# Moving a sample's recurrent-state update from ScalarE and VectorE to GpSimd

## The chip, the core and the metric

The kernel runs on one core of one Trainium2 chip. The number that counts is the device time of one launch in microseconds (us). Engines are named as the profile names them: PE is TensorE (PEld its weight loads), DVE is VectorE, ACT is ScalarE, POOL is GpSimd, SP is SyncE. Each engine runs its instructions in the order in which they stand in its queue; an instruction that waits for a semaphore holds back everything behind it on its engine.

## The reference, cut to what matters

One layer of a decoder step: 256 prompt tokens and 8 sample tokens share all weights. The mixer half has three branches; two of them (HGRN2 with 8 heads of 128x128, GLA with 4 heads of 128x256) are gated linear recurrences. For the samples there is one new token, so the recurrence is a single step from a given state:

```
S_t = diag(f_t) S_{t-1} + k_t v_t^T       # per sample and head; S is dk x dv
o_t = S_t^T q_t
```

Both the new state S_t (an output, for every sample and head) and o_t are wanted. The rest (norms, projections, an MLP, the prompt's recurrence in chunks) is matrix work over the 264 tokens.

## The kernel before, in words

**Main stream.** All projections are computed as weight-stationary matmuls in an fp32 scheme of three products (lines 602, 603, 604): each weight block `raw` is loaded by SP, rounded to `whi` by ACT (line 109) and its remainder `wlo` made by DVE (line 106, `wlo = raw - whi`, two SBUF inputs), then PE runs three 128x264 matmuls for each 128x128 block. The unit of the stream is the *granule*: 8 weight blocks of 128x128, so 24 matmuls on PE. `now` counts granules while the program is written out; the whole program has 578. Splits run two granules ahead, loads five.

**Side work.** Everything else in the mixer half is written between granules by generators that hand over after each piece: `mixer_r(G)` (queue `bg`) for the prompt's recurrence of a group G, and `samples_r(G)` (queue `bs`) for the samples of the same group. There are three groups, in this order: two HGRN halves (four heads each, dv = 128) and GLA (dv = 256). Small matmuls of the side work are gathered into *slots* between two granules: line 633 (prompt levels), line 640 (samples), line 342 (the modulation's weights).

**The samples' step.** `samples_r` goes through `steps`: 8 steps in an HGRN group (one per sample), 16 in GLA (two per sample). The tile of a step is 128x512 (`st`, the state; `vbc`, the value row, spread over all partitions from DRAM scratch `vs_d`). In each step:
- POOL issues the load of the state two steps ahead (line 1029, `fetch`; 4 buffers) and of the value row one step ahead (line 1035, `values`; 2 buffers);
- ACT scales the state by the decay `fs`, one instruction per head (line 1055);
- DVE adds the outer product, `st = v * k + st`, one instruction per head (line 1057), where the per-partition scalar is a column of `k` (`G.k`, a [128, 4, 264] tile);
- POOL issues the store of the state (line 1058);
- after a sample's last step, `samples.append((now[0], ...))`; `slot` takes it `AGE` = 2 granules later and writes its products `S_t^T q` (line 640) to PE.

With 4 state buffers, the load of step n+2 goes into the buffer of step n-2, so it waits until the product of that step has been read by PE.

**What reads k and who gets its buffer.** `k` is also read by the prompt's side, last in `mul(kd, kd, k[:, :, 0:NP])` (line 1170). Tiles `b` come from a pool of 28 buffers, and a buffer is given to a new tile when the last reader of the old one is done. In the built program of both kernels the tile `qd` of the first group (written by ACT's exponential at line 1163, multiplied by q on DVE in a `mul`, which the profile shows at its helper's line 100, and read by PE in the products at line 1176) lies at the same address as that group's `k`. Line 1176 stands on PE at granule 127 in both kernels.

**What sets the order.** PE, SP and POOL keep the order in which the program is written. For DVE and ACT a scheduler chooses it when the kernel is built, so a change of their work moves their other instructions as well.

Of the kernel before, what the change touches and what calls it, by code (L numbers as in the profile page):

```python
# [10 lines left out]
AF = mybir.ActivationFunctionType  # L11
ALU = mybir.AluOpType
# [3 lines left out]
P = 128  # L16
D = 2048
KT = D // P
NP = 256
# [32 lines left out]
FETCHED = 3  # L52
AGE = 2
ADA_LAND = 4


@with_exitstack
def hybrid_step_kernel(
# [8 lines left out]
    nc = tc.nc  # L67
    V, S, T = nc.vector, nc.scalar, nc.tensor
# [17 lines left out]
    def blk(shape=None, dt=F32):  # L86
        shape = shape or [P, 4, NT]
        return blkp.tile(shape, dt, tag="b", name=nm("b"))
# [4 lines left out]
    def tmp(shape, tag, bufs=2):  # L93
        return tp.tile(shape, F32, tag=tag, name=nm(tag), bufs=bufs)
# [4 lines left out]
    def mul(o, a, b):  # L99
        V.tensor_tensor(o, a, b, op=ALU.mult)  # L100
# [72 lines left out]
    def rstd_small(ms, scale, out):  # L173

        n, w = out.shape
        xx, aa = tmp([P, 16], "sx")[0:n, 0:w], tmp([P, 16], "sa")[0:n, 0:w]
        c = 0
        for m in ms if isinstance(ms, list) else [ms]:
            V.tensor_scalar(xx[:, c:c + m.shape[1]], m, scale, EPS, ALU.mult, ALU.add)
            c += m.shape[1]  # L180
        V.tensor_scalar(out.bitcast(I32), xx.bitcast(I32), -0.5, 1597463007.0, ALU.mult, ALU.add)
        for _ in range(3):
            mul(aa, out, out)
            V.scalar_tensor_tensor(aa, aa, -0.5, xx, ALU.mult, ALU.mult)
            V.scalar_tensor_tensor(out, aa, 1.5, out, ALU.add, ALU.mult)
# [102 lines left out]
    class Rounds:  # L288
# [27 lines left out]
        def due(self):  # L316
            if self.ws:
                return self.full() and now[0] >= self.at + ADA_LAND
            return self.done is not None and not self.todo and now[0] >= self.at + 2 * ADA_LAND

# [35 lines left out]
    now = [0]  # L356
# [250 lines left out]
    levels, samples = [], []  # L607
# [406 lines left out]
    def samples_r(G):  # L1014

        dv = G.dv
        nj, nh = dv // P, 512 // dv
        q, k, g = G.q, G.k, G.g
        fs = tmp([P, 4, NS], "fs")
        S.activation(fs, g[:, :, NP:NT], AF.Exp)  # L1020
        qm = blk([P, 4, NS, 32])
        mul(qm, q[:, :, NP:NT].unsqueeze(3).to_broadcast([P, 4, NS, 32]),
            delta.rearrange("p (b c) -> p b c", b=NS).unsqueeze(1).to_broadcast([P, 4, NS, 32]))
        steps = [(b, h) for b in range(NS) for h in range(0, 4, nh)]
        ahead, vals = [], []

        def fetch(b, h):
            st = tmp([P, nh, dv], "st", ST_BUFS)
            nc.gpsimd.dma_start(st, G.s_in(b, h, nh))
            ahead.append((st, now[0]))  # L1030

        def values(b, h):
            v = tmp([P, 4, P], "vbc", VB_BUFS)
            r0 = 4 * nj * b + h * nj
            nc.gpsimd.dma_start(v, vs_d[G.i, r0:r0 + 4, :].partition_broadcast(P))
            vals.append((v.rearrange("p (h j) v -> p h (j v)", h=nh), now[0]))

        for s in steps[0:2]:
            fetch(*s)
            yield  # L1040
        values(*steps[0])
        yield
        os_ = tmp([P, dv], f"os{G.i}", 1)
        sts = []
        for n, (b, h0) in enumerate(steps):
            if n + 2 < len(steps):

                yield lambda: len(sts) + sum(len(x[3]) for x in samples) <= ST_BUFS - 3
                fetch(*steps[n + 2])
            if n + 1 < len(steps):  # L1050
                values(*steps[n + 1])
            yield lambda: now[0] >= max(ahead[0][1] + FETCHED, vals[0][1] + FETCHED - 1)
            st, v = ahead.pop(0)[0], vals.pop(0)[0]
            for i in range(nh):
                S.activation(st[:, i, :], st[:, i, :], AF.Copy, scale=fs[:, h0 + i, b:b + 1])  # L1055
            for i in range(nh):
                V.scalar_tensor_tensor(st[:, i, :], v[:, i, :], k[:, h0 + i, NP + b:NP + b + 1], st[:, i, :], ALU.mult, ALU.add)  # L1057
            nc.gpsimd.dma_start(G.s_out(b, h0, nh), st)  # L1058
            sts.append(st)
            if h0 + nh == 4:  # L1060
                samples.append((now[0], (G, qm, os_), b, sts))
                sts = []
            yield
        yield lambda: not samples
        yield READY
        ss, rr = tmp([P, 1], "sss", 1), tmp([P, 1], "srr", 1)
        S.activation(tmp([P, dv], "vt"), os_, AF.Square, accum_out=ss)
        rstd_small(ss, 1.0 / dv, rr)
        S.activation(os_, os_, AF.Copy, scale=rr)
        G.os = os_  # L1070
        yield

    def mixer_r(G):
# [18 lines left out]
        q, k, g = G.q, G.k, G.g  # L1092

        bs.g.append(samples_r(G))


# [625 lines left out]
```

## Time and profile before

| | |
|---|---|
| time, median of 3 runs | 1942.22 us (1941.23 to 1944.57) |
| span of the profiled execution | 1942.9 us; no other time of that execution is given |
| PE busy | 1903.4 us (98%) |
| DVE busy | 1186.1 us (61%) |
| ACT busy | 1006.5 us (52%) |
| POOL busy | 83.9 us (4%), 142 instructions, most of them DMA issues |
| the samples' work, lines 1029 to 1058 and 640 | from 377 to 850 us of the span |

How to read it: "busy" is the union of the instructions of an engine. A wait is put down to the instruction that waits and to the last thing that it waited for. The chain of work that ended last is followed back from the last instruction; idle time of an engine that is not on it costs nothing. A clock of 1.00 is the full TensorE clock.

### The profile page before, as it was taken

Reading aid. Unit: us, or ns where it says so; the run is one execution under the profiler, and the core shown is the slowest. Engines: PE = TensorE matmul, PEld = TensorE weight load, DVE = VectorE, ACT = ScalarE, POOL = GpSimd, SP = SyncE. Lnnn points to the kernel's source line nnn. Section 1 sums busy time; section 2 is a strip of 40 time slices with the busy share of each in tenths; the row PEclk is TensorE's granted clock in tenths of the full one; section 3 lists DMA queues with packets and bytes.
Section 4 is the critical chain, followed back from the end, with each engine's and each line's share of the span. In section 5 each row is a group of like instructions: output and inputs, shape, how many; then the busy total and the mean of one; then the engine's idle time right before and its main releaser. Section 6 shows DMA issues by size and latency. Waiting matters only on the chain.

```text
span 1942.9 us, 42324 instructions
## 1 busy us (share of the span) xinstructions
PE 1903.4 (98%) x17080; PEld 1812.1 (93%) x17080; DVE 1186.1 (61%) x2103; ACT 1006.5 (52%) x1825; POOL 83.9 (4%) x142
## 2 busy tenths in 40 slices
PE   6999999998999999999999999999999999999998
PEld 5989999988999998999999988999999999999997
DVE  4566667686578695565555666545556555555665
ACT  5444454665666765544444556444444545454444
POOL 1000000001001112200000010000000000000000
PEclk9999999999999999999999999999999999999999
DMA  9897786688588688987777846776566555555552
GB/s 317 299 337 247 249 287 213 214 250 276 175 262 290 214 258 283 306 266 249 253 256 233 300 129 195 229 226 199 178 182 184 179 180 184 177 183 182 179 183 99
DMA packets 339380, 442.06 MB, mean 228 GB/s; under 512 B 14930, under 2 KB 281024, under 8 KB 339184
## 3 DMA queue, kind: packets, MB, share of 16 engines
q1 hardware_dynamic: 329120, 409.62, 65.5%
q0 software_dynamic: 8992, 28.48, 4.6%
q8 instruction: 134, 2.20, 0.5%
q10 hardware_dynamic: 1072, 1.25, 0.2%
q14 instruction: 62, 0.51, 0.1%
HBM read 427.60 MB, written 11.70 MB: 226 GB/s over the span
## 4 chain that ended last, share of the span: by engine, by line
PE 95%; DMA 2%; issue 1%; ACT 1%; DVE 1%; POOL 0%; SPq 0%; ACTq 0%; DVEq 0%; POOLq 0%
PE mm L602 29%; PE mm L603 29%; PE mm L604 28%; PE ada L342 3%; PE ada L274 1%; PE sm L633 1%; PE sm L780 1%; DMA raw<-in_w_in_dram 1%; PE sm L640 0%; DMA b<-in_x_prompt_dram 0%; DMA vbc<-vs_d 0%; DVE wlo L106 0%; DMA b<-in_w_ada_dram 0%; ACT gt L1515 0%; PE sm L1176 0%
## 5 line engine op out<-in xcount | busy, mean ns | idle before, releaser
L602 PE MATMUL mm<-b,whi 128*128 128x264 f32 x4624 | 1326.6, 287 | 7.5 <-ACT b L109 3.5
L603 PE MATMUL mm<-b,whi 128*128 128x264 f32 x4624 | 1317.8, 285 | 0.8 <-DVE b L106 0.8
L604 PE MATMUL mm<-b,wlo 128*128 128x264 f32 x4624 | 1314.5, 284 | 1.4 <-issue 0.7
L106 DVE TENSOR_TENSOR wlo<-raw,whi 128x512 fp32r<-128x512 f32 x1136 | 775.5, 689 | 572.0 <-ACT whi L109 570.0
L109 ACT CAST whi<-raw 128x512 fp32r<-128x512 f32 x1136 | 695.4, 618 | 730.6 <-PE mm L603 654.5
L602 PEld LDWEIGHTS mm<-b,whi 128*128 128x128 f32 x4624 | 872.3, 189 | 49.1 <-issue 26.2
L604 PEld LDWEIGHTS mm<-b,wlo 128*128 128x128 f32 x4624 | 872.5, 189 | 2.2 <-DVE wlo L106 1.1
L603 PEld LDWEIGHTS mm<-b,whi 128*128 128x128 f32 x4624 | 872.2, 189 | 1.4 <-DVE b L106 1.3
L103 DVE TENSOR_TENSOR b<-b,mm 128x528 f32<-128x528 f32 (+1 forms) x137 | 95.7, 700 | 42.7 <-PE mm L604 42.7
L1057 DVE SCALAR_TENSOR_TENSOR st<-vbc,b,st 128x128 f32<-128x128 f32 (+1 forms) x96 | 34.1, 389 | 51.1 <-DMA vbc<-vs_d 44.2
L1055 ACT ACTIVATE st<-st,fs 128x128 f32<-128x128 f32 (+1 forms) x96 | 37.0, 430 | 53.0 <-DMA st<-in_state_hgrn_dram 27.0
L274 PE MATMUL ada<-b,cT 128*32 128x256 f32 (+1 forms) x640 | 35.7, 361 | 7.2 <-DMA b<-in_w_ada_dram 7.0
L342 PE MATMUL ada<-araw,cT 128*32 128x512 f32 x296 | 39.9, 601 | 0.0
L274 PEld LDWEIGHTS ada<-b,cT 128*32 128x32 f32 x640 | 18.2, 115 | 19.7 <-issue 6.4
L100 DVE TENSOR_TENSOR b<-b,b 128x512 f32<-128x512 f32 (+1 forms) x47 | 34.1, 740 | 1.4 <-ACT b L1165 0.9
L1058 POOL DMA_DIRECT2D out_dram<-st x32 | 23.5, 735 | 156.6 <-DVE st L1057 150.8
L342 PE MATMUL ada<-b,cT 128*32 128x512 f32 x216 | 26.2, 593 | 0.0
L106 DVE TENSOR_TENSOR b<-gt,b 128x528 fp32r<-128x528 f32 x32 | 22.7, 708 | 3.9 <-ACT whi L109 0.9
L106 DVE TENSOR_TENSOR b<-b 128x1024 f32<-128x1024 f32 (+1 forms) x24 | 24.3, 1016 | 0.0
L109 ACT CAST whi<-araw 128x512 fp32r<-128x512 f32 x20 | 12.4, 621 | 20.7 <-PE mm L603 19.0
L100 DVE TENSOR_TENSOR gt<-vt 128x528 f32<-128x528 f32 x32 | 22.4, 701 | 0.9 <-ACT vt L1581 0.9
L1587 ACT ACTIVATE b<-vt 128x528 fp32r<-128x528 f32 x32 | 20.7, 647 | 1.0
(339 smaller groups left out, 825.2 us busy)
## 6 DMA issues: line engine op xcount, KB each, us to landing
raw<-in_w_in_dram SPq DMA_DIRECT2D x232, 512.0 KB, 4.7
raw<-in_w_mlp_up_dram SPq DMA_DIRECT2D x128, 512.0 KB, 3.7
raw<-in_w_mlp_down_dram SPq DMA_DIRECT2D x128, 512.0 KB, 3.6
b<-in_w_ada_dram SPq DMA_DIRECT2D x102, 512.0 KB, 6.4
araw<-in_w_ada_dram SPq DMA_DIRECT2D x74, 512.0 KB, 6.0
raw<-in_w_branch_dram SPq DMA_DIRECT2D x48, 512.0 KB, 4.5
raw<-in_w_out_dram SPq DMA_DIRECT2D x32, 512.0 KB, 3.9
b<-in_w_ada_dram SPq DMA_DIRECT2D x32, 256.0 KB, 5.7
```

What stands on the lines that cost most here:

```text
L100: V.tensor_tensor(o, a, b, op=ALU.mult)
L103: V.tensor_tensor(o, a, b, op=ALU.add)
L106: V.tensor_tensor(o, a, b, op=ALU.subtract)
L109: S.copy(hi, src)
L274: T.matmul(acc[32 * j:32 * j + 32, 0:n], cT[:, k, :], w[:, n * j:n * j + n], start=k == 0, stop=k == KT - 1)
L342: T.matmul(self.acc[32 * j:32 * j + 32, :], cT[:, k, :], ws[j // 2][:, j % 2 * 512:j % 2 * 512 + 512], start=k == 0, stop=k == KT - 1)
L602: T.matmul(o, a, xh(k + j), start=first and j == 0, stop=False)
L603: T.matmul(o, a, xl(k + j), start=False, stop=False)
L604: T.matmul(o, b, xh(k + j), start=False, stop=last and j == n - 1)
L1055: S.activation(st[:, i, :], st[:, i, :], AF.Copy, scale=fs[:, h0 + i, b:b + 1])
L1057: V.scalar_tensor_tensor(st[:, i, :], v[:, i, :], k[:, h0 + i, NP + b:NP + b + 1], st[:, i, :], ALU.mult, ALU.add)
L1058: nc.gpsimd.dma_start(G.s_out(b, h0, nh), st)
```

## The change

The 96 ACT and 96 DVE instructions of lines 1055 and 1057 go. Each of the 32 steps issues three POOL instructions on 128x512 instead: the state times the decay (one decay per head, broadcast along dv), the value row times k (the same, and written in place over the value row), and their sum. A sample's products are written one granule later (`POOL_AGE`). All line numbers behind line 54 rise by one.

```
+POOL_AGE = 1
...
             st, v = ahead.pop(0)[0], vals.pop(0)[0]
-            for i in range(nh):
-                S.activation(st[:, i, :], st[:, i, :], AF.Copy, scale=fs[:, h0 + i, b:b + 1])
-            for i in range(nh):
-                V.scalar_tensor_tensor(st[:, i, :], v[:, i, :], k[:, h0 + i, NP + b:NP + b + 1], st[:, i, :], ALU.mult, ALU.add)
+            hs = slice(h0, h0 + nh)
+            nc.gpsimd.tensor_tensor(st, st, fs[:, hs, b:b + 1].to_broadcast([P, nh, dv]), op=ALU.mult)
+            nc.gpsimd.tensor_tensor(v, v, k[:, hs, NP + b:NP + b + 1].to_broadcast([P, nh, dv]), op=ALU.mult)
+            nc.gpsimd.tensor_tensor(st, st, v, op=ALU.add)
             nc.gpsimd.dma_start(G.s_out(b, h0, nh), st)
             sts.append(st)
             if h0 + nh == 4:
-                samples.append((now[0], (G, qm, os_), b, sts))
+                samples.append((now[0] + POOL_AGE, (G, qm, os_), b, sts))
```

POOL's queue of the first group, the last steps. `st_...` are state tiles, `vbc_...` value rows, `out_dram` the states' output. Before, from the load of step 6 (the seventh state) on:

```order
L1029 DMA st_5855<-in_state_hgrn_dram 128x4x128
L1035 DMA vbc_5857<-vs_d 128x512
L1058 DMA out_dram<-st_5602 128x4x128
L1029 DMA st_6097<-in_state_hgrn_dram 128x4x128
L1035 DMA vbc_6099<-vs_d 128x512
L1058 DMA out_dram<-st_5842 128x4x128
L1035 DMA vbc_6110<-vs_d 128x512
L1058 DMA out_dram<-st_5855 128x4x128
L1058 DMA out_dram<-st_6097 128x4x128
```

And now, from the load of step 6 (`st_6058`) to the store of step 5 (`st_5783`); `b_4812` is k:

```order
L1030 DMA st_6058<-in_state_hgrn_dram 128x4x128
L1036 DMA vbc_6060<-vs_d 128x512
L1056 TENSOR_TENSOR st_5775<-st_5775,fs_5014 128x512
L1057 TENSOR_TENSOR vbc_5785<-vbc_5785,b_4812 128x512
L1058 TENSOR_TENSOR st_5775<-st_5775,vbc_5785 128x512
L1059 DMA out_dram<-st_5775 128x4x128
L1030 DMA st_6066<-in_state_hgrn_dram 128x4x128
L1036 DMA vbc_6068<-vs_d 128x512
L1056 TENSOR_TENSOR st_5783<-st_5783,fs_5014 128x512
L1057 TENSOR_TENSOR vbc_6060<-vbc_6060,b_4812 128x512
L1058 TENSOR_TENSOR st_5783<-st_5783,vbc_6060 128x512
L1059 DMA out_dram<-st_5783 128x4x128
```

Behind that come one more value row, the three operations of step 6, its store, the three operations of step 7, and its store. The arithmetic now stands between the DMA issues: steps 4 to 7 are all behind the load of step 6, which waits for a product on PE (that of step 2, in the slot at granule 124).

ACT's queue where `qd` is written, with the semaphores that each instruction waits for. Before (`b_1018_6089` is qd, `b_27_172` the cumulated log decay, `st_1020_6097` the state of step 7):

```order
L1165 ACTIVATE b_1017_6088<-b_1017_6088 128x1024 [waits DVE_49]
L109 CAST whi_1012_6078<-raw_997_5937 128x512 [waits DMAHW2_49,PE_49,Activation_49]
L1055 ACTIVATE st_1020_6097<-st_1020_6097,fs_868_5014 128x128 [waits DMASW5_49,DMASW1_49]
L1055 ACTIVATE st_1020_6097<-st_1020_6097,fs_868_5014 128x128 x3
L109 CAST whi_1014_6082<-raw_997_5937 128x512 [waits PE_49,Activation_49]
L109 CAST whi_1025_6140<-raw_1002_5982 128x512 [waits DMAHW3_49,PE_49,Activation_49]
L109 CAST whi_1027_6144<-raw_1002_5982 128x512 [waits PE_49,Activation_49]
L109 CAST whi_1031_6176<-raw_1007_6016 128x512 [waits DMAHW4_49,PE_49,Activation_49]
L1163 ACTIVATE b_1018_6089<-b_27_172 128x512 [waits DVE_49]
L109 CAST whi_1033_6180<-raw_1007_6016 128x512 [waits PE_49,Activation_49]
```

And now (`b_1015_6050` is qd):

```order
L1166 ACTIVATE b_1014_6049<-b_1014_6049 128x1024 [waits DVE_49]
L110 CAST whi_1009_6039<-raw_994_5909 128x512 [waits DMAHW2_49,PE_49,Activation_49]
L110 CAST whi_1011_6043<-raw_994_5909 128x512 [waits PE_49,Activation_49]
L110 CAST whi_1023_6098<-raw_999_5943 128x512 [waits DMAHW3_49,PE_49,Activation_49]
L110 CAST whi_1025_6102<-raw_999_5943 128x512 [waits PE_49,Activation_49]
L110 CAST whi_1029_6134<-raw_1004_5977 128x512 [waits DMAHW4_49,PE_49,Activation_49]
L110 CAST whi_1031_6138<-raw_1004_5977 128x512 [waits PE_49,Activation_49]
L1164 ACTIVATE b_1015_6050<-b_27_172 128x512 [waits DVE_49,Pool_49]
```

The states' scalings are gone from between the casts, and the exponential that writes qd waits for POOL as well. In the built program the value that it waits for is that of the second operation of step 7 (line 1057 in the new numbering, the last reader of k).

The places of the sample products on PE, in granules: before 114, 119, 124, 128, 129, 133 in the first group, 154 to 169 in the second, 192 to 227 in GLA; now 118, 124, 129, 133 in the first, 154 to 174 in the second, 194 to 236 in GLA (six or seven granules apart, the last two at 234 and 236).

## The prediction

> **What bounds the kernel now.** I read the page's busy line and its chain first, then busy time by stage, then the waits of the stages in which the samples run, then the one wait that matters instruction by instruction.
>
> ```profile
> PE 1903.4 (98%) x17080; PEld 1812.1 (93%) x17080; DVE 1186.1 (61%) x2103; ACT 1006.5 (52%) x1825; POOL 83.9 (4%) x142
> PE 95%; DMA 2%; issue 1%; ACT 1%; DVE 1%; POOL 0%; SPq 0%; ACTq 0%; DVEq 0%; POOLq 0%
> ```
>
> PE is the bound. Work taken from ACT and DVE pays only where PE waits for them. The stages with sample work, with the gaps between (columns: stretch, length, busy time and count of PE, PEld, DVE, ACT, POOL, then clock, DMA share, GB/s):
>
> ```profile
> 377.00:480.00 103.00, 98.04 (x1183) 89.33 (x1181) 79.16 (x145) 66.72 (x132) 16.75 (x26) 1.00 0.82 262
> 480.00:531.00 51.00, 50.34 (x431) 47.67 (x432) 22.74 (x55) 31.29 (x72) 1.54 (x3) 0.93 0.57 181
> 531.00:626.00 95.00, 94.96 (x1206) 88.27 (x1204) 74.52 (x141) 64.02 (x128) 16.05 (x25) 1.00 0.84 269
> 626.00:669.00 43.00, 43.00 (x371) 40.98 (x370) 22.56 (x56) 30.14 (x71) 1.75 (x3) 1.00 0.69 222
> 669.00:760.00 91.00, 91.00 (x1151) 86.05 (x1150) 75.71 (x123) 56.91 (x105) 14.56 (x23) 1.00 0.84 275
> 760.00:850.00 90.00, 89.48 (x722) 81.19 (x721) 47.89 (x94) 49.45 (x105) 19.42 (x29) 1.00 0.88 294
> ```
>
> PE is busy for 466.8 of these 473 us, so 6.2 us is all that PE loses here by waiting. Now who waits for whom between 377 and 850:
>
> ```profile
> PE sm L1176 <- DVE b L100: 4.7, 1, 4.7
> PE mm L604 <- issue: 0.7, 1, 0.7
> PE mm L604 <- DVE wlo L106: 0.7, 2, 0.4
> DVE st L1057 <- DMA vbc<-vs_d: 44.2, 14, 6.3
> ACT st L1055 <- DMA st<-in_state_hgrn_dram: 27.0, 7, 7.9
> ACT st L1055 <- DMA st<-in_state_gla_dram: 25.9, 10, 6.9
> ACT b L1163 <- DVE st L1057: 2.1, 1, 2.1
> ```
>
> DVE and ACT do stand still for 97 us behind loads, in front of their splits, and PE hardly notices, with one exception of 4.7 us: the products at line 1176, granule 127. The chain shows what is behind it (start, length, what):
>
> ```profile
> 468.46 7.77 DMA vbc<-vs_d
> ...
> 478.94 0.28 DVE st L1057
> 479.22 0.02 issue
> 479.24 0.64 ACT b L1163
> ...
> 479.91 0.70 DVE b L100
> ...
> 480.66 2.08 PE sm L1176 x8
> ```
>
> A value row lands; DVE finishes the last steps' line 1057, the last readers of k; only then may ACT write qd, which has k's buffer; DVE multiplies by q; PE goes on. So in the old kernel too, the first group's last sample step stands on PE's path. From the end of line 1057 (479.22) to PE (480.66) it is 1.44 us. PE had been there since 475.94 (the row below), and it came back at half clock:
>
> ```profile
> 475.66 0.28 PE L604 MATMUL mm<-b,wlo 128*128 128x264 f32 x1
> 475.00:480.00 5.00, 0.94 (x8) 0.73 (x7) 3.65 (x9) 1.38 (x3) 1.25 (x2) 1.00 1.06 407
> 480.00:485.00 5.00, 4.34 (x20) 4.35 (x21) 1.20 (x2) 0.97 (x2) 0.26 (x1) 0.50 0.92 299
> 485.00:490.00 5.00, 5.00 (x64) 4.66 (x64) 1.67 (x3) 1.81 (x3) 0.00 (x0) 0.82 0.08 17
> ```
>
> **The change, part by part.** *Removed:* the instructions of lines 1055 and 1057.
>
> ```profile
> L1057 DVE SCALAR_TENSOR_TENSOR st<-vbc,b,st 128x128 f32<-128x128 f32 (+1 forms) x96 | 34.1, 389 | 51.1 <-DMA vbc<-vs_d 44.2
> L1055 ACT ACTIVATE st<-st,fs 128x128 f32<-128x128 f32 (+1 forms) x96 | 37.0, 430 | 53.0 <-DMA st<-in_state_hgrn_dram 27.0
> ```
>
> 34.1 us of DVE, 37.0 us of ACT and the 97 us of standing still go. Nearly all of it lies beside PE's work: apart from line 1176 PE idles 6.2 - 4.7 = 1.5 us in these stages. Worth 0 to 1.5 us; I take 0.7.
>
> *Added:* 96 POOL operations of 128x512. The trace has smaller ones:
>
> ```profile
> L1518 POOL TENSOR_TENSOR b<-xsn,b 128x32 fp32r<-128x32 f32 x4 | 1.0, 251 | 0.3
> L1455 POOL TENSOR_TENSOR os<-gs,xsT 128x128 f32<-128x128 f32 x1 | 0.5, 451 | 115.2 <-DVE gs L100 115.2
> ```
>
> From 32 to 128 elements it is 200 ns, 2.08 ns an element; 451 + 384 * 2.08 gives 1.25 us (estimate; 1.1 to 1.4). 96 * 1.25 = 120 us on an engine that is busy 4%. The set-up instruction that stood once on POOL ahead of its first arithmetic now stands ahead of step 0; that step's product is at granule 118, six granules of 3.4 us (below) before 466, so at 446, against loads from 377 on: hidden.
>
> [...]
>
> *The wait that grows.* Steps 4 to 7 of the first group now stand on POOL behind the load of step 6, and that waits for PE's product at granule 124. The old kernel has a load at the same place, and its time tells when the slot's product is done:
>
> ```profile
> 465.48 0.76 POOL L1058 DMA_DIRECT2D out_dram<-st  x1 [13.31 <-DVE st L1057]
> 466.43 0.75 POOL L1029 DMA_DIRECT2D st<-in_state_hgrn_dram  x1 [0.20 <-PE sm L640]
> 467.17 0.55 POOL L1035 DMA_DIRECT2D vbc<-vs_d  x1
> ```
>
> Call 466.43 T. PE reaches line 1176 at T + 9.5 (three granules later, in both kernels). From T, POOL must do, one after the other, until the second operation of step 7 has read k: two state loads, three value rows, three stores (2 * 0.75 + 3 * 0.55 + 3 * 0.76 = 5.4 us) and 3 + 3 + 3 + 2 = 11 operations (13.8 us): 19.2 us if nothing waits. The landing of the loads (min, median, max; value rows, then states):
>
> ```profile
> DMA to landing us min/median/max: 3.7/6.7/10.0
> DMA to landing us min/median/max: 3.1/6.2/9.7
> ```
>
> The last value row is issued behind step 5's store, 0.75 + 0.55 + 3.75 + 0.76 + 0.75 + 0.55 + 3.75 + 0.76 = 11.6 us after T, and lands 6.7 us (median) to 7.8 us (the row of the chain above, at this very place) later: T + 18.3 to 19.4, and its operation ends at T + 19.6 to 20.7. I take the second, because the DMA queues are as full there (share 1.06), and add 0.8 us for contention with DVE (below): T + 21.5. Then 1.44 us of ACT and DVE as before: PE goes on at T + 22.9 = 489.4, against 480.66. **PE loses 8.7 us more.** Nothing covers it: PE's order is fixed, and what stands behind line 1176 on PE waits with it, as do ACT's casts behind the exponential; PE makes up nothing later, being the bound. Ends: no wait for landings and 1.17 us an operation (5.4 + 12.9 + 1.44 = 19.7, so +5.5); landing after 10 us and each operation behind one 0.69 us split (+15).
>
> *The clock.* It dips once behind the wait, in both kernels; a wait of 13 us instead of 5 costs the same dip. I take 0, bounds -1 to +1.
>
> *The other products.* One granule later, each after its own chain on POOL. Two slots of GLA, five granules apart:
>
> ```profile
> 788.10 0.57 PE sm L640 x8
> 805.18 0.57 PE sm L640 x8
> ```
>
> 17.1 us, 3.4 a granule. Between two samples of GLA POOL has two loads, two rows, a store and six operations: 1.5 + 1.1 + 0.8 + 7.5 = 10.9 us, with a row's landing hidden behind the first three operations; the products are now 6 or 7 granules apart, 20 to 24 us. The last two are 2 granules apart, but step 14 waits for the product at 227, nine granules (31 us) ahead of the last, and needs some 24 us by the same rows. They hold. The tightest is GLA's third: POOL's queue has the store of the prompt's final state in front of step 5, which waits for a sum after PE's granule 205, and the product stands at 208, 10 us later, against about 7 us of work. I take 0, upper end 3 us. SP's own queue gains waits for such stores ahead of loads of modulation weights, five granules before PE needs what is behind them: 0.
>
> *DVE's second reader.* POOL's operations read SBUF beside DVE's splits. The only overlap in the trace, two equal POOL casts, the second 30 ns behind the start of a DVE operation with two SBUF inputs:
>
> ```profile
> 1156.33 0.21 POOL L1517 CAST b<-xsn 128x32 fp32r<-128x32 f32 x1
> 1156.81 0.46 POOL L1517 CAST b<-xsn 128x32 fp32r<-128x32 f32 x1
> 1156.78 0.43 DVE L106 TENSOR_TENSOR b<-vt,b 128x256 fp32r<-128x256 f32 x1 [0.47 <-ACT b L109]
> ```
>
> The second took 0.25 us more and ended 0.06 us after DVE's: it looks held until DVE was done. One pair is thin, but with splits of 0.69 us it puts a few tenths on each of the six operations of steps 4 and 5 (later DVE has run dry, since PE stands); part is hidden by the landings, hence the 0.8. The other way round POOL could hold DVE: in the densest stage, 531 to 626, 24 operations of 1.25 us are 30 us; DVE was busy 74.5 of 95 us and waited for value rows besides, and loses 32 * 0.30 of its own. 74.5 - 9.7 + 30 = 95: full only if every operation held DVE for its whole length, and DVE has idle time and PSUM work. I take 0.7 us on PE in all (it cancels the relief), ends 0 and 5.
>
> [...]
>
> *Sum.* 8.7 - 0.7 + 0.7 + 0 = +8.7 us on a span of 1942.9, 1951.6; the span stands 0.7 us above the median of the runs, so **1951 us**.
>
> **Rivals.** (1) *Held up on both engines:* DVE's back-to-back splits let POOL in late and POOL's operations make the splits late. For it: the cast above, and DVE busy 75.7 of 91 us from 669 on. Against: PE bore 97 us of standing still on DVE and ACT. The wait at line 1176 then goes to its end (+15) and PE waits 3 to 10 us elsewhere: 1960 to 1968.
>
> (2) *Short chain:* landings hidden and POOL unhindered, +5.5 at line 1176, and the full relief of 1.5: 1946, not to be told from no change (a measurement of this kernel tells about 0.2%, 3.9 us, from nothing).
>
> (3) *Faster:* the wait at line 1176 disappears, because DVE and ACT no longer stand behind loads ahead of qd. For it: a vbc wait is in the old chain. It decides at T + 9.5 - 1.4 = T + 8.1: if POOL's last reader of k were done by then, PE would gain the 4.7 us, about 3 us of clock dip (5 * 0.50 + 5 * 0.18 us of clock missing in the two rows above) and 1.5: 1942.9 - 9.2 - 0.7 = 1933. Against: 19.2 us of POOL's own work must fit into 8.1.
>
> **How the numbers follow.** Forecast, wait grown by 6 to 14 us: 0.69. Rival 1: 0.14. Rival 2: 0.11. Rival 3: 0.06. Slower by over 0.2% is above 1946.1: the forecast and rival 1, 0.83; same 0.11; faster 0.06. Range 1945 to 1961: from rival 2's time to the lower end of rival 1.
>
> **What would show it.** Right: between two groups of splits near 475 us PE waits some 13 us at line 1177 for DVE, DVE for ACT's line 1164, ACT for POOL's 1057; POOL's queue runs without a gap of more than a few us from the product at granule 124 on; POOL's operations read 1.1 to 1.4 us; PE idles nowhere else by more than 1 us. Wrong: POOL's operations much shorter than 1 us, qd written before step 7, PE waiting at line 641 or for `wlo`, or DVE's 128x512 splits over 0.8 us in the mean.

## The result, and the profile after

The changed kernel takes 1956.49 us (median; 1956.34 to 1962.35), the old one, run beside it, 1943.39 us: ratio 1.0073, 95% interval 1.0059 to 1.0087. It is slower, by 13 us, of which the forecast of 1951 (1945 to 1961) had 8.7. The profiled execution spans 1954.5 us, against 1942.9. Line numbers move by the lines that a kernel adds: the products at granule 127 are line 1175 to 1180, the helper of the splits is line 106 or 107, that of a `mul` 100 or 101.

From the page: the busy line and the engines' shares of the chain.

```profile
PE 1903.7 (97%) x17080; PEld 1812.5 (93%) x17080; DVE 1249.3 (64%) x2006; ACT 979.3 (50%) x1729; POOL 225.3 (12%) x238
PE 94%; DMA 1%; DVE 1%; POOL 1%; ACT 1%; issue 1%; SPq 0%; DVEq 0%; ACTq 0%; POOLq 0%
```

PE's busy time is the same (1903.7, 1903.4); the span grew by 11.6 us, so PE's idle time did (39.5 to 50.8). DVE has 97 instructions fewer and 63 us more of busy time. Busy time by stage, columns as before the change:

```profile
377.00:480.00 103.00, 97.95 (x1179) 89.36 (x1177) 90.17 (x110) 58.65 (x101) 50.86 (x43) 0.99 0.79 258
480.00:531.00 51.00, 42.09 (x365) 39.37 (x366) 25.13 (x48) 25.50 (x62) 9.39 (x9) 0.86 0.50 152
531.00:626.00 95.00, 94.22 (x1175) 88.85 (x1177) 80.80 (x107) 55.30 (x95) 32.60 (x35) 1.00 0.81 257
...
669.00:760.00 91.00, 89.59 (x1103) 84.20 (x1102) 80.68 (x117) 53.14 (x95) 29.46 (x29) 1.00 0.77 251
```

PE idles 8.9 us between 480 and 531, where it idled 0.7, and 5.1 us before 480, where it was 5.0. From 531 to 626 and 669 to 760 it loses 0.8 and 1.4, where it lost nothing. The waits of 377 to 850 name the places (us in total, times, longest):

```profile
PE sm L1177 <- DVE b L101: 14.0, 1, 14.0
PE mm L605 <- DVE wlo L107: 1.3, 3, 0.6
PE sm L634 <- DVE b L101: 0.8, 1, 0.8
ACT b L1164 <- POOL vbc L1057: 10.8, 1, 10.8
POOL vbc L1057 <- DMA vbc<-vs_d: 0.8, 1, 0.8
```

One wait has grown, the one at granule 127, from 4.7 to 14.0. ACT's line 1164, which writes qd into k's buffer, waits for POOL's line 1057, the last reader of k. The loads that cost DVE 44.2 us of standing still now cost POOL 0.8. The way to that wait, from the timelines of POOL, ACT, DVE and PE (start, length, engine, line):

```profile
465.47 0.75 POOL L1030 DMA_DIRECT2D st<-in_state_hgrn_dram  x1 [7.64 <-PE sm L641]
...
472.94 1.99 POOL L1056 TENSOR_TENSOR st<-st,fs 128x512 f32<-128x512 f32 x1
...
484.56 1.06 POOL L1056 TENSOR_TENSOR st<-st,fs 128x512 f32<-128x512 f32 x1
485.58 1.05 POOL L1057 TENSOR_TENSOR vbc<-vbc,b 128x512 f32<-128x512 f32 x1
486.71 1.60 POOL L1058 TENSOR_TENSOR st<-st,vbc 128x512 f32<-128x512 f32 x1
486.66 0.63 ACT L1164 ACTIVATE b<-b 128x512 f32<-128x512 f32 x1 [10.83 <-POOL vbc L1057]
487.33 1.53 DVE L101 TENSOR_TENSOR b<-b,b 128x512 f32<-128x512 f32 x1
488.91 2.08 PE L1177 MATMUL sm<-b,b 128*128 128x128 f32 x8 [13.96 <-DVE b L101]
```

With T = 465.47 (the load of step 6, released by PE's product at granule 124) the last reader of k ends at T + 21.2 and PE goes on at T + 23.4; PE had been there since T + 9.5. DVE's multiplication by q took 1.53 us instead of 0.70, beside POOL's last operation.

The second thing the traces show is DVE's splits from 377 to 900, first of the old kernel, then of the new one with POOL's operations (busy, mean ns of one):

```profile
L106 DVE TENSOR_TENSOR wlo<-raw,whi 128x512 fp32r<-128x512 f32 x289 | 193.1, 686 | 99.0 <-ACT whi L109 98.5
```

```profile
L107 DVE TENSOR_TENSOR wlo<-raw,whi 128x512 fp32r<-128x512 f32 x282 | 255.6, 932 | 95.8 <-ACT whi L110 94.1 <-PE sm L641 0.8 <-PE mm L604 0.6
L1056 POOL TENSOR_TENSOR st<-st,fs 128x512 f32<-128x512 f32 x32 | 51.9, 1620 | 27.8 <-ACT fs L1021 27.4
L1058 POOL TENSOR_TENSOR st<-st,vbc 128x512 f32<-128x512 f32 x32 | 50.9, 1592 | 2.5
L1057 POOL TENSOR_TENSOR vbc<-vbc,b 128x512 f32<-128x512 f32 x32 | 38.4, 1200 | 2.1 <-DMA vbc<-vs_d 2.1
```

A split takes 932 ns in the mean instead of 686. It is not a slow-down of all, but a few that stand long: 54 of the 282 take over 0.8 us, and the median is 0.69. DVE beside POOL's step 6 (POOL's three operations there: 479.71 to 480.77, 480.72 to 481.77, 481.86 to 483.46):

```profile
479.14 3.19 DVE L107 TENSOR_TENSOR wlo<-raw,whi 128x512 fp32r<-128x512 f32 x1
...
483.93 3.26 DVE L107 TENSOR_TENSOR wlo<-raw,whi 128x512 fp32r<-128x512 f32 x1
```

The first split ended at 482.33, 0.56 us after POOL's second operation; the third at 487.19, 0.56 us after the second operation of step 7. DVE got one split in at the small gap behind POOL's second operation, one behind the third, one behind the second of step 7: three in 8.04 us, which take 2.1 us by themselves.

### The profile page after: what moved, and what is told of

Read it like the earlier page. It is cut to its first block, busy times and chain, and to the rows that moved or that the text cites. A ratio compares the mean times of both kernels' runs of the same rounds, so it can differ in the third digit from the quotient of the medians.

```text
span 1954.5 us, 42163 instructions
## 1 busy us (share of the span) xinstructions
PE 1903.7 (97%) x17080; PEld 1812.5 (93%) x17080; DVE 1249.3 (64%) x2006; ACT 979.3 (50%) x1729; POOL 225.3 (12%) x238
## 3 DMA queue, kind: packets, MB, share of 16 engines
q10 hardware_dynamic: 1072, 1.25, 0.2%
## 4 chain that ended last, share of the span: by engine, by line
PE 94%; DMA 1%; DVE 1%; POOL 1%; ACT 1%; issue 1%; SPq 0%; DVEq 0%; ACTq 0%; POOLq 0%
PE mm L603 29%; PE mm L604 28%; PE mm L605 28%; PE ada L343 3%; PE ada L275 1%; DMA b<-in_w_ada_dram 1%; PE sm L634 1%; PE sm L781 1%; DVE wlo L107 1%; PE sm L641 0%; DMA b<-in_x_prompt_dram 0%; DVE b L107 0%; POOL st L1056 0%; ACT whi L110 0%; POOL st L1058 0%
## 5 line engine op out<-in xcount | busy, mean ns | idle before, releaser
L107 DVE TENSOR_TENSOR wlo<-raw,whi 128x512 fp32r<-128x512 f32 x1136 | 843.4, 751 | 574.8 <-ACT whi L110 571.4
L1056 POOL TENSOR_TENSOR st<-st,fs 128x512 f32<-128x512 f32 x32 | 51.9, 1620 | 27.8 <-ACT fs L1021 27.4
L1058 POOL TENSOR_TENSOR st<-st,vbc 128x512 f32<-128x512 f32 x32 | 50.9, 1592 | 2.5
L101 DVE TENSOR_TENSOR b<-b,b 128x512 f32<-128x512 f32 (+1 forms) x47 | 44.3, 965 | 2.8 <-ACT b L1166 2.1
L1057 POOL TENSOR_TENSOR vbc<-vbc,b 128x512 f32<-128x512 f32 x32 | 38.4, 1200 | 2.1 <-DMA vbc<-vs_d 2.1
L107 DVE TENSOR_TENSOR b<-b 128x1024 f32<-128x1024 f32 (+1 forms) x24 | 30.5, 1273 | 0.0
```

The lines of the kernel that those rows point to most:

```text
L107: V.tensor_tensor(o, a, b, op=ALU.subtract)
L1056: nc.gpsimd.tensor_tensor(st, st, fs[:, hs, b:b + 1].to_broadcast([P, nh, dv]), op=ALU.mult)
L1057: nc.gpsimd.tensor_tensor(v, v, k[:, hs, NP + b:NP + b + 1].to_broadcast([P, nh, dv]), op=ALU.mult)
L1058: nc.gpsimd.tensor_tensor(st, st, v, op=ALU.add)
```

## The experiments

Two theories on the 13 us. **A:** the wait of qd for k's last reader sets it. **B:** POOL's operations hold DVE and its splits come late for PE; the wait at granule 127 only covers that. In the table "copy" means that k's sample columns are copied to a small tile, from which the samples read, so that k's buffer is free early; PE's idle time is 483.00 us less its busy time from 377 to 860 in the profiled execution. Each ratio is to the old kernel as it ran beside that run, and the old kernel's row has the range of its medians. The idle times of e2 and e7 are to be read with care: their profiled executions took 1941.84 and 1933.39 us, 3.7 us above and 3.4 us below the medians.

From e5 on, the recorded expectations give the letters A and B to the theories that each of them names; in e5, e7 and e8 their A is what is B here.

| label | arithmetic | copy | products later | us, median | ratio to before (95%) | PE idle, 377 to 860 |
|---|---|---|---|---|---|---|
| before | ACT, DVE | no | no | 1943.39 to 1944.72 | 1 | 6.2 |
| after | POOL | no | yes | 1956.49 | 1.0073 (1.0059 to 1.0087) | 16.2 |
| e1 | POOL | yes | yes | 1956.97 | 1.0067 (1.0055 to 1.0079) | 12.9 |
| e2 | ACT, DVE | yes | no | 1938.11 | 0.9970 (0.9959 to 0.9981) | 3.0 |
| e3 | POOL | no | no | 1957.51 | 1.0066 (1.0054 to 1.0078) | 16.7 |
| e4 | ACT, DVE | no | yes | 1958.30 | 1.0075 (1.0061 to 1.0089) | 18.1 |
| e5 | fills on POOL | yes | yes | 1936.53 | 0.9958 (0.9946 to 0.9971) | 1.9 |
| e6 | ACT, DVE | yes | yes | 1951.28 | 1.0035 (1.0024 to 1.0046) | 11.6 |
| e7 | one operation on POOL, DVE | yes | no | 1936.77 | 0.9960 (0.9948 to 0.9972) | 0.1 |
| e8 | POOL | yes | no | 1951.11 | 1.0037 (1.0025 to 1.0049) | 12.3 |
| e9 | POOL, fills added | no | yes | 1960.55 | 1.0080 (1.0068 to 1.0093) | 21.5 |
| e10 | two on POOL, add on DVE | yes | no | 1940.11 | 0.9979 (0.9969 to 0.9989) | 4.0 |
| e11 | one operation on POOL, DVE | no | no | 1943.63 | 0.9997 (0.9988 to 1.0005) | 6.8 |

**e1, the wait for k's buffer taken away from the new kernel.**

```diff
+        ks = tmp([P, 4, NS], "fs")
+        V.tensor_copy(ks, k[:, :, NP:NT])
...
-            nc.gpsimd.tensor_tensor(v, v, k[:, hs, NP + b:NP + b + 1]...
+            nc.gpsimd.tensor_tensor(v, v, ks[:, hs, b:b + 1]...
```

> The changed kernel, but the eight sample columns of k are copied once per group into a small tile (128x32, DVE), and POOL reads the copy; so k's buffer is free for qd as soon as the prompt's side is done with it. Everything else, the slots on PE too, is as in the changed kernel. Theory A (PE's loss is the wait of qd for POOL's last reader of k): the 14.0 us at the first group's attention products fall to 0 to 5 us (what is left is DVE being held by POOL when it multiplies qd), the clock dip shrinks with it, and the time is 9 to 17 us below the changed kernel, 1939 to 1947. Theory B (the loss is POOL and DVE holding each other, wherever the buffers lie): the wait stays at 8 us or more and the time above 1950.

The waits of PE from 377 to 850, and the longest of the new ones with DVE's and POOL's rows ahead of it:

```profile
PE mm L605 <- DVE wlo L107: 9.2, 4, 4.2
PE sm L1179 <- DVE b L101: 2.0, 1, 2.0
```

```profile
403.67 3.96 DVE L101 TENSOR_TENSOR b<-b,b 128x512 f32<-128x512 f32 x2
405.00 1.06 POOL L1058 TENSOR_TENSOR st<-st,fs 128x512 f32<-128x512 f32 x1
406.02 1.05 POOL L1059 TENSOR_TENSOR vbc<-vbc,fs 128x512 f32<-128x512 f32 x1
407.15 1.60 POOL L1060 TENSOR_TENSOR st<-st,vbc 128x512 f32<-128x512 f32 x1
407.55 2.28 DVE L107 TENSOR_TENSOR b<-b 128x1024 f32<-128x1024 f32 x1
410.49 0.39 PE L605 MATMUL mm<-b,wlo 128*128 128x264 f32 x1 [3.82 <-DVE wlo L107]
```

The wait of 14.0 fell to 2.0, as A says, but the time did not move (1956.97): PE now waits 9.2 us for splits. Two DVE operations of 0.69 us each took 3.96 us together beside POOL's first two, the next 2.28 instead of 1.22, and PE stood 3.82 us for the split behind them. A names the wait rightly and fails on the time; B has the time (above 1950) and not the wait (8 us or more).

**e2, the same copy in the old kernel** (DVE's line 1057 reads `ks`).

> The kernel before, with the same small copy of k's sample columns, read by DVE's line 1057. Theory A: the 4.7 us at the first group's attention products and most of the 3 us of half clock behind them go: 1934 to 1938. If the wait there comes from the loads in front of DVE and ACT alone and not from k's buffer, it stays at 3 us or more and the time within 0.2% of before (1939 to 1947). The difference between this kernel and the one with POOL's arithmetic and the copy is what POOL's arithmetic costs without the buffer: A says 2 to 9 us, B says 10 us or more.

1938.11, at the upper end of A's 1934 to 1938: the 4.7 us at granule 127 and the clock dip behind it are gone (the clock is 1.00 from 475 to 495, where the old kernel's went down to 0.50). So with the copy POOL's arithmetic and the delay together cost 1956.97 - 1938.11 = 19 us, which is B's size (10 or more) and not A's (2 to 9).

**e3, the new kernel with the products at their old granules** (`POOL_AGE = 0`).

> The changed kernel without the granule of delay (POOL_AGE = 0): products where they were before. Step 6's load then waits for the product at granule 119, and only step 7's for that at 124, so behind that product POOL has 14 us of work instead of 21 us before its last read of k. Theory A: the wait shrinks by about 7 us to 6 to 8 us, and the time is 6 to 8 us below the changed kernel, 1948 to 1951; none of the sample products waits for POOL by more than 1 us. Theory B: as slow as the changed kernel or slower, 1955 or more, since POOL does as much arithmetic in less time.

```profile
PE sm L1177 <- DVE b L101: 8.7, 2, 7.1
PE mm L605 <- DVE wlo L107: 5.8, 6, 1.7
```

The long wait shrinks to 7.1 us, as A says, and the time does not: 1957.51 is in B's range.

**e4, the old kernel with the products one granule later** (`samples.append((now[0] + 1, ...`).

> The kernel before (ACT and DVE update the states), with the products one granule later alone. Step 6's load now waits for granule 124 instead of 119, POOL's store of step 5 stands in front of step 7's value row and waits for DVE, which waits for step 5's value row. Theory A: the last reader of k is DVE's step 7, two landings behind the product, about 18 us after it instead of 13; the wait grows from 4.7 to 8 to 12 us and the time is 3 to 8 us above before, 1946 to 1951. Theory B: no change from before, within 0.2%, as no POOL arithmetic is added.

```profile
PE sm L1176 <- DVE b L100: 8.9, 1, 8.9
PE mm L604 <- DVE wlo L106: 3.5, 5, 1.4
```

The wait is A's, the time is nobody's: 1958.3, where A said 1946 to 1951 and B no change. The delay alone costs as much as the whole change, POOL's arithmetic alone (e3) too. The two do not add up.

The next four all have the copy. **e5: fills in place of the three operations.** This kernel leaves out the state update.

```diff
-            nc.gpsimd.tensor_tensor(st, st, fs...
-            nc.gpsimd.tensor_tensor(v, v, ks...
-            nc.gpsimd.tensor_tensor(st, st, v, op=ALU.add)
+            for x in (st, st, v, v, st, st, st):
+                nc.gpsimd.memset(x, 1.0)
```

> GpSimd's three operations of a step are replaced by seven fills of the same tiles (they write SBUF and read nothing; estimate 0.5 us each from the kernel's fill of 1024 elements, so about as long as the three together); the state update is left out, all loads, stores and products stay, and k's sample columns are copied. Theory A (what costs time is that GpSimd's reads of SBUF hold DVE): DVE's splits keep 0.69 us, PE waits for wlo less than 1.5 us in all, and the time is that of the old arithmetic with the copy, 1936 to 1942. Theory B (what costs time is the one-after-the-other chain on GpSimd and the later products): 1953 to 1960, as with the three operations.

```profile
L107 DVE TENSOR_TENSOR wlo<-raw,whi 128x512 fp32r<-128x512 f32 x293 | 199.0, 688 | 161.8 <-ACT whi L110 160.3 <-PE sm L641 0.8 <-issue 0.3
L1059 POOL MEMSET st<- 128x512 f32 x160 | 84.7, 529 | 5.7 <-DMA st<-in_state_hgrn_dram 0.2
```

Seven fills are 3.7 us a step, as long as the three operations (1.06, 1.05 and 1.60 in the rows of e1). Splits are back at 688 ns (906 in e1), PE idles 1.9 us of 483, and the time is 1936.53: 20.4 us less than e1, with the same loads, stores and later products. What the fills lack is the arithmetic with its read of SBUF; no run here parts these two, so that it is the reads which hold DVE, as A has it, is not shown.

**e6: the old arithmetic, products one granule later.**

> The old arithmetic on ACT and DVE, with the copy of k's sample columns, and the products one granule later. Theory A (the delay costs only through the wait for k's last reader): no wait over 2 us at the attention products, 1936 to 1942. Theory B (the delay costs by itself, since loads and stores come later and ACT and DVE stand still longer): 1946 to 1955.

Waits from 377 to 850, first with the products at their old places (e2), then later (e6):

```profile
DVE st L1059 <- DMA vbc<-vs_d: 48.4, 17, 6.1
```

```profile
DVE st L1059 <- DMA vbc<-vs_d: 67.0, 17, 8.9
PE mm L604 <- DVE wlo L106: 4.5, 5, 1.1
```

1951.28, theory B's time here: the delay costs 13 us by itself. Each load waits for an earlier sample's product, so it is issued later; DVE stands 67.0 us behind value rows instead of 48.4, in front of splits. PE's waits for splits are the largest part of its 11.6 us idle, 4.5 us; the rest is spread over several other places. In e5, where nothing on DVE or ACT stands behind a load, the same delay shows no cost: its time is not told apart from those of e2 and e7, which have no delay.

**e7: one operation on POOL, in place of ACT's four scalings.**

```diff
-            for i in range(nh):
-                S.activation(st[:, i, :], st[:, i, :], AF.Copy, scale=fs[:, h0 + i, b:b + 1])
+            nc.gpsimd.tensor_tensor(st, st, fs[:, h0:h0 + nh, b:b + 1].to_broadcast([P, nh, dv]), op=ALU.mult)
```

> As the old arithmetic with the copy, but the states' scaling (four ACT instructions a step) is one GpSimd operation of 1.06 us; DVE keeps line 1057. Theory A with a cost in proportion (1.06 of 3.75 us of GpSimd's work): a third of the 13 to 19 us, 1942 to 1945. Theory A with slack (only what holds DVE longer than PE's lead counts): 1936 to 1940. Theory B: DVE now waits for GpSimd in each step, in front of its splits, 1945 to 1955.

```profile
377.00:860.00 483.00, 482.94 (x5223) 450.73 (x5222) 349.42 (x638) 282.60 (x533) 117.51 (x137) 1.00 0.80 265
L106 DVE TENSOR_TENSOR wlo<-raw,whi 128x512 fp32r<-128x512 f32 x297 | 204.2, 702 | 92.1 <-ACT whi L109 88.6 <-PE mm L603 2.7
```

1936.77: PE idles 0.06 us of 483, and the time equals that of e5, in which nobody does the update. DVE's splits take 702 ns in the mean (689 in e2), so there are holds, but those of one operation lie within PE's lead (the time from the end of a split to the first matmul that reads it): no split from 377 to 860 ended less than 0.7 us ahead of PE.

**e8: all three operations, no delay** (e1 with `POOL_AGE = 0`).

> The three GpSimd operations, the copy of k's sample columns, and no delay of the products. Theory A: no long wait at the attention products, PE waits 6 to 12 us in all for wlo, 1951 to 1959. Theory B: with the delay gone, 1940 to 1948.

```profile
PE mm L605 <- DVE wlo L107: 9.8, 7, 3.9
```

1951.11, 13 us over e2, and 9.8 of PE's 12.3 us idle are waits for splits: the hold without the delay and without the buffer's wait, at the size expected for it (6 to 12 us of waits; the time is at the lower end).

**e9: POOL's chain in the new kernel made longer.**

```diff
+            if G.i == 0 and 4 <= n <= 6:
+                for _ in range(3):
+                    nc.gpsimd.memset(v, 0.0)
```

> The changed kernel with three more GpSimd fills of 0.53 us behind each of the steps 4, 5 and 6 of the first group (9 * 0.53 = 4.8 us more between the load of step 6 and the last reader of k); nothing is left out. Chain theory (GpSimd's own work behind that load sets the wait): the wait at the attention products grows from 14.0 to 18 or 19 us, 1960 to 1962. [...]

```profile
PE sm L1180 <- DVE b L101: 17.2, 1, 17.2
```

```profile
480.63 1.88 DVE L107 TENSOR_TENSOR wlo<-raw,whi 128x512 fp32r<-128x512 f32 x3
484.74 1.26 POOL L1058 TENSOR_TENSOR st<-st,vbc 128x512 f32<-128x512 f32 x1
```

The wait grows by 3.2 us, less than the 4 to 5 expected for the chain. The median is 4.1 us higher, but the ratios (1.0080, 1.0073) are not told apart, so it is the wait that decides. Its growth is 1.6 us short of the 4.8 added, because POOL's operations are shorter: the first two of step 5, held in the changed kernel (1.99 and 1.48 us), take 1.06 and 1.05 here, and DVE gets its next three splits done beside the fills (1.88 us, against 8.04) and then stands idle, so that step 6's addition takes 1.26 instead of 1.60. POOL's own chain sets this wait.

**e10: two operations on POOL, the addition on DVE** (`add(st, st, v)`, one operation a step).

> Copy of k's sample columns, no delay; GpSimd does the two multiplications of a step (2.1 us), DVE the addition (one 128x512 operation). Holding in proportion to GpSimd's time: nothing seen with one operation, so 1938 to 1942. Slack theory (PE bears a hold of DVE up to its lead, and GpSimd's runs of operations without a break are what exceeds it): waits for wlo of 1 to 5 us, 1940 to 1948. Rival (DVE now waits for GpSimd's two operations ahead of its splits): 1948 or more.

```profile
PE mm L604 <- DVE wlo L106: 2.9, 3, 1.6
```

1940.11, between e7 and e8, and inside the ranges of two of the three theories; that PE waits 2.9 us for splits is what the slack theory says. With POOL's one, two and three operations a step (1.06, 2.1 and 3.7 us) PE idles 0.1, 4.0 and 12.3 us, and the medians are 1936.77, 1940.11 and 1951.11: the price grows faster than the time on POOL. The three kernels differ in what DVE does as well, so this is no pure count of operations.

**e11: e7 without the copy.**

> The old kernel with the states' scaling as one GpSimd operation a step, without the copy of k's sample columns. Buffer theory: DVE's line 1057 still reads k until step 7, the wait at the attention products is 3 to 6 us, 1940 to 1946. Rival (with ACT free of the scalings the last reader is early enough): wait under 1.5 us, 1934 to 1939.

```profile
PE sm L1175 <- DVE b L100: 6.6, 1, 6.6
```

1943.63: the buffer's wait is back (6.6 us, above the 3 to 6 expected) and takes the 7 us of e7. The copy is worth 5.6 us in the old kernel (e2), 7.0 in e4 (e6), 6.4 in e3 (e8) and 6.9 here. Only in the changed kernel (e1) it is worth nothing.

e7 beats both kernels (0.9960, 0.9948 to 0.9972); from e2 (0.9970, 0.9959 to 0.9981) it is not told apart.

## Why the prediction was right, and where not

*The wait that grows: right, by its own sum.* Eleven operations took 14.6 us, where 13.8 + 0.8 of contention was forecast. The last reader of k ended at T + 21.2 (T + 21.5), PE went on at T + 23.4 (T + 22.9), the growth was 9.3 us (8.7). That it came so close is in part luck, as terms inside the sum were off and cancelled. No operation of this stretch waited for its value row (+1.5 had been put in). The multiplications are shorter than the 1.25 forecast (1.06), and the addition, with two whole tiles as inputs, is longer (1.60 beside DVE's splits, 1.26 in e9 where DVE is idle) and is followed by 0.3 us before its store; so the sign "1.1 to 1.4 us" holds for neither in this kernel. Two operations of step 5 were held by DVE, for 1.36 us (1.99 and 1.48 against 1.06; 0.8 had been put in). The way from the last reader to PE took 2.3 us instead of 1.44, as DVE's multiplication by q was held too. And DVE had not run dry in steps 6 and 7, as the prediction thought: its splits stood until 487.19, and it was POOL's multiplications there that went on unhindered (1.06 and 1.05).

*The clock: right.* PE's busy time under a lowered clock is about the same: 4.34 us at 0.50 and 5.00 at 0.82 before (3.1 us lost), and now

```profile
485.00:490.00 5.00, 1.09 (x5) 1.09 (x6) 3.72 (x2) 0.63 (x1) 4.03 (x4) 0.50 0.54 164
490.00:495.00 5.00, 5.00 (x48) 4.61 (x48) 0.00 (x0) 1.17 (x2) 0.00 (x0) 0.53 0.22 71
```

1.09 * 0.50 + 5.00 * 0.47 = 2.9 us.

*The other products: right.* No wait of PE at a sample product (line 641) appears.

*Relief and DVE's second reader: small in the sum, wrong as a reading.* Together they were put at nothing. PE's other waits from 377 to 860 grew from 1.5 to 2.2 us, so 0.7 was missed; another 1.3 us of idle time lies outside that stretch. But two signs named for "wrong" came true, splits over 0.8 us in the mean (932 ns) and, for 1.3 us, PE waiting for `wlo`: operations do hold DVE, for two in a row (3.19 us for the split of 479.14). And the experiments show that the long wait hides this: e1 takes it away and is no shorter, with 9.2 us of waits for splits in its place (rival 1's mechanism). Why does the changed kernel itself bear the holds with 1.3 us of waiting, where e1 pays 9.2? For the two long waits of e1 (3.82 and 4.21 us) the traces show which engine held the other. First e1, then the changed kernel, then both at the second place, in the same order:

```profile
393.00 6.44 POOL L1058 TENSOR_TENSOR st<-st,fs 128x512 f32<-128x512 f32 x1 [12.65 <-ACT fs L1021]
```

```profile
394.17 11.71 POOL L1056 TENSOR_TENSOR st<-st,fs 128x512 f32<-128x512 f32 x1 [12.63 <-ACT fs L1021]
```

```profile
627.73 0.59 PE L605 MATMUL mm<-b,wlo 128*128 128x264 f32 x1 [4.21 <-DVE wlo L107]
```

```profile
627.66 4.94 POOL L1056 TENSOR_TENSOR st<-st,fs 128x512 f32<-128x512 f32 x1
```

In the changed kernel POOL's first operation was kept out until 405.88, and by then DVE had finished the two splits that PE needed next, at 402.03 and 404.97, 4.2 and 2.7 us ahead of PE. In e1 POOL's first operation was done at 399.44, and the next ones held DVE in front of the same two splits: one ended at 403.75, 1.3 us ahead of PE, the other at 410.43, with PE waiting for it (e8 has the same wait, 3.87 us). At the second place POOL stood for 4.94 us in the changed kernel, and in e1 DVE did, at a split (2.90 us from 617.15) and a multiplication (3.73 us from 622.27). Why POOL got in at one time and not at the other is not shown; nor is the reason why the delay adds 6 us to e8.

*The base: mis-sized, and half of the miss.* The span came out 2.9 us over the forecast (1954.5, 1951.6). The other 2.7 us are the last step: the forecast took the median 0.7 us below the span. An execution's time is about 2 us over its span (1956.55 against 1954.5 here, 1943.06 against 1941.2 in e11), so the profiled execution of before took some 1944.9 (an estimate). With more runs the old kernel's median is 1943.39 to 1944.72; the 1942.22 of three runs, to which the sum was tied, was low.

*Rivals.* The faster one (3) needed k's last reader by T + 8.1; it came at T + 21.2. The short chain (2) needed no hindrance; POOL was held in step 5.

## What to carry to other kernels

Before work moves to an idle engine, look at which buffers it reads and who writes them next: an in-order chain there becomes the release time of the buffer (T + 21.2 here), and copying the 32 columns that it needs was worth 5.6 to 7.0 us in four kernels, and nothing in the changed one, where the holds took its place. An engine's free time is not free if its operations hold up another engine: one operation of 1.06 us a step cost nothing (e7), three in a row 13 us (e8), fills of the same length nothing (e5). And undo a change one part at a time, in both directions: here each half alone cost as much as the whole, so "without this wait it would be as before" would have been wrong.

## What the hardware showed that was not expected

The hold goes both ways and lasts longer than one instruction. DVE's split of 479.14, 0.69 us by itself, took 3.19 us, until 0.56 us after POOL's second operation. POOL's first operation took 11.71 us in the changed kernel (its row stands above, at 394.17), and in e7:

```profile
393.21 1.19 POOL L1056 TENSOR_TENSOR st<-st,fs 128x512 f32<-128x512 f32 x1 [12.65 <-ACT fs L1020]
```

The same operation is the first in both, so the difference is no one-time set-up. In the changed kernel DVE ran operations with SBUF inputs without a break from before 394.17, and POOL ended at 405.88, 1.00 us (about one operation's length, 1.06) after the start of DVE's next operation that has a PSUM input:

```profile
404.88 0.49 DVE L1002 TENSOR_SCALAR b<-sm,vec 128x264 f32<-128x264 f32 x1
```

In these rows either engine kept the other out while its own instructions followed one another at once. What lets the other in is not settled: in e1 the same operation was done at 399.44 while the operations of DVE around it had all their inputs in SBUF. Nor does a record tell where a hold begins: the split that stood until 482.33 starts at 479.14, 0.57 us ahead of the first POOL operation that held it, while POOL was issuing a value row.
